# Seven half-size products for eight behind the attention of a gated hybrid block, with fused token steps

## The chip, the cores and the metric

The kernel runs on one core of a Trainium2 chip (trn2). The metric is the device time of one execution, in microseconds (us); lower is better. The engines are TensorE (PE; its weight loads are shown apart as PEld), VectorE (DVE), ScalarE (ACT), GpSimd (POOL) and SyncE (SP), which issues the DMAs of this kernel. Each engine works through its own queue in order; semaphores order the queues among each other.

## The reference, cut to what matters

The input is x of 2048 tokens by 1024 features, the output has the same shape, all float32.

```python
h = rms_norm(x, norm_gain)
proj = h @ w_in                                # 1024 x 8448
qa, ka, va, qb, kb, vb, ga, gb, mg = split(proj)
ya = banded_attention(qa, ka, va, window 128, sink) * silu(ga)    # 512 wide
yb = (three dilated groups of attention, joined by their denominators) * silu(gb)   # 512 wide
gates = sigmoid(mg + b_merge)                  # two gates, each 1024 wide
merged = gates[0] * (ya @ w_branch_a) + gates[1] * (yb @ w_branch_b)
out = x + merged @ w_out
```

## The kernel before

**Precision.** Every large product is made of float16 parts. An operand is split into a high part (`XH`, `wh`) and a low part (`XL`, `wl`), and each product is three matmuls, high by high, high by low and low by high. The high part is a scaled copy by ACT (`w_hi`, L215), the low part is a subtraction by DVE (`w_lo`, L221). `XH` and `XL` hold h transposed, with the features on partitions, and stay in SBUF through the gates.

**Stages.** First x is loaded, normed and turned (`x_turn` L447, `x_hi` L450, `x_lo` L454), and gate chunks 0 and 1 run on the way. Then come 14 attention units of 8 steps each (112 steps, `NPAIR`). Two are A units, twelve are B units. A step does the projections of two sets of 128 tokens (`Pair`, matmuls at L617), their head norms (L635 to L699), the logits (L767), the softmax (`maxima` L782, `exps` L790, `hi` L795, `lo` L799) and the values (L816). `a_merge` and `b_merge_q` join the results, and `YPart` turns 512 tokens of 128 features, multiplies them with the silu gate (L882), takes their maximum (L887) and stores them in DRAM (`ytd`).

**Fills.** A gate chunk is 128 columns of the gate weights, a whole chunk being four quarters of 24 matmuls of 512 columns (`g_step`, L288). Chunks 0 to 7 are the silu gates: a tanh by ACT (L350) and a product by DVE (L357), stored in `gtd` and loaded again by `YPart.load`. Chunks 8 to 11 are merge gates (tanh at L353 only, stored in `mgd`) for output column blocks 6 and 7. The list `FILLS` says in which of the 112 steps a quarter runs between the attention's products, and chunk 8 has steps 116 and 118, behind the attention:

```python
FILLS = ((2, None, (2, 3, 4, 5)), (3, 0, (8, 9, 10, 12)), (4, 1, (17, 19, 20, 21)), ...
```

A chunk needs its own weight preparation: load, gain by POOL (L303), square, norm (L173 and L180 to L188), high and low part (L329, L333).

**The order by hand.** The queues hold what the program emits, in the order of emission. `at(t, f)` puts a piece of work on a heap under a planned time, counted in steps; `until(t)` emits what is due. PE's products are emitted in sequence, and the work of the other engines falls between them as the heap says.

**Behind the attention.** The merge gates of block 0 run in plain order (`mg_step`). All of y is loaded from DRAM and split into `YH` and `YL` (L1122 to L1124). Then, for output blocks dc = 1 to 7 and 0, and for four quarters of 512 tokens each, PE makes the two merge gates (only for dc 1 to 5; the others come from `mgd`) and the two branch products of 12 matmuls each, DVE joins them (L1204, L1205, L1208), and the result is stored in DRAM (`mtd`):

```python
tproj(ps, wh, wl, 256, q, 4, YH, YL, 4 * k)
V.scalar_tensor_tensor(gs[k][:], gs[k][:], 1.0, ps[:], OP.add, OP.mult)
```

The output stage loads `mtd` into `M` and makes 2 x 16 products of 24 matmuls (L1254); DVE adds x (L1257), and SyncE stores the result.

Of the kernel before, what the change touches and what calls it, by code (L numbers as in the profile page):

```python
# [39 lines left out]
VSC = 2.0 ** -20  # L40
SX = 2.0 ** 10
# [31 lines left out]
G_PREP = (5.907, 6.8, 7.032, 7.43, 7.58, 7.73, 7.88)  # L73
# [9 lines left out]
FILLS = ((2, None, (2, 3, 4, 5)), (3, 0, (8, 9, 10, 12)), (4, 1, (17, 19, 20, 21)), (5, 2, (24, 25, 26, 27)), (6, 3, (33, 35, 36, 37)), (7, 4, (40, 41, 42, 44)), (9, 6, (58, 59, 60, 62)), (10, 7, (64, 65, 66, 68)), (11, 10, (88, 89, 90, 92)), (8, 13, (116, 116, 118, 118)))  # L83
# [8 lines left out]
def block_kernel(tc, x, w_units, w_gate, w_mrg, w_out, w_bra, gain, qkg, sink, bias_a, bias_b, b_merge, out):  # L92
# [10 lines left out]
    wp = es.enter_context(tc.tile_pool(name="wp", bufs=2))  # L103
# [43 lines left out]

    def w_load(u, parts=(0, 1, 2, 3)):
        if u not in wtiles:
            wtiles[u] = [raw_tile()]  # L150
        raw = wtiles[u][0]
        src = w_units[u] if u < NU else w_mrg[u - NU]
        for i in parts:
            nc.sync.dma_start(out=raw[:, 2 * i:2 * i + 2, :], in_=src[:, 2 * i:2 * i + 2, :])
# [36 lines left out]
    def w_square(u, i):  # L191
        raw = wtiles[u][0]
        if i == 0:
            wtiles[u] += [wp.tile([128, NCH, 384], F16, name="wh"), wp.tile([128, NCH, 384], F16, name="wl"),
                          sm.tile([128, 4], F32, name="wsq")]
# [64 lines left out]
    ytd = [dr.tile([128, S], F32, name=f"ytd{c}") for c in range(8)]  # L260
    gtd = [dr.tile([128, S], F32, name=f"gtd{c}") for c in range(8)]
    mgd = {k: dr.tile([128, S], F32, name=f"mgd{k}") for k in (0, 1, 12, 13, 14, 15)}
# [4 lines left out]
    gp = main.enter_context(tc.tile_pool(name="gp", bufs=1))  # L267
# [37 lines left out]
    def g_square(c):  # L305
        pool = gp if c > 1 else sp0
        bufs = 1 if c > 1 else 2
        gh = pool.tile([128, NCH, 128], F16, name="gh", bufs=bufs)
        gl = pool.tile([128, NCH, 128], F16, name="gl", bufs=bufs)
# [26 lines left out]
    def g_step(c, q):  # L336
# [3 lines left out]
        m = None if c < 8 else 4 + c  # L340
        ps = pj_p.tile([128, 512], F32, name="pj")
        return tproj_list(ps, gh, gl, 0, q), gate_steps(ps, c, q, ih, m)

    def gate_steps(ps, c, q, ih, m):
# [10 lines left out]
        def gate():  # L355
            if m is None:
                V.scalar_tensor_tensor(th[0][:], th[0][:], 1.0, ps[:], OP.add, OP.mult)  # L357

# [677 lines left out]
    for c, u, slots in FILLS:  # L1036
        for q, k in enumerate(slots):
            fill.setdefault(k, []).append((g_step, c, q))
        if c == 2:
            continue  # L1040
# [293 lines left out]
```

## Time and profile before

| | |
|---|---|
| median of 3 runs | 2015.74 us (2012.35 to 2018.49) |
| span of the profiled execution | 2015.2 us |
| PE busy | 1965.1 us, 98% of the span, 17666 matmuls |
| DVE busy | 1265.5 us, 63% |
| ACT busy | 1004.8 us, 50% |
| POOL busy | 839.3 us, 42% |
| DMA | 276.97 MB, mean 137 GB/s |

No other time is known for the profiled execution than its span from the first to the last instruction. The page cuts the span into 40 slices of 50.4 us; each digit is a busy share in tenths. In a group of instructions the columns are the sum of the busy time, the mean in ns of one, and the idle time of the engine before them with what ended it. In a table of windows each engine has its busy time in that stretch and the number of its instructions; the last three columns are PE's granted clock (1.00 is full), the share of the DMA engines and their rate. The attention's steps lie between about 82 and 1384 us; what is behind them is called the tail.

### The profile page before, as it was taken

Reading aid. Unit: us, or ns where it says so; the run is one execution under the profiler, and the core shown is the slowest. Engines: PE = TensorE matmul, PEld = TensorE weight load, DVE = VectorE, ACT = ScalarE, POOL = GpSimd, SP = SyncE. Lnnn points to the kernel's source line nnn. Section 1 sums busy time; section 2 is a strip of 40 time slices with the busy share of each in tenths; the row PEclk is TensorE's granted clock in tenths of the full one; section 3 lists DMA queues with packets and bytes.
Section 4 is the critical chain, followed back from the end, with each engine's and each line's share of the span. In section 5 each row is a group of like instructions: output and inputs, shape, how many; then the busy total and the mean of one; then the engine's idle time right before and its main releaser. Section 6 shows DMA issues by size and latency. Waiting matters only on the chain.

```text
span 2015.2 us, 47585 instructions
## 1 busy us (share of the span) xinstructions
PE 1965.1 (98%) x17666; PEld 1399.8 (69%) x17666; DVE 1265.5 (63%) x3456; ACT 1004.8 (50%) x2357; POOL 839.3 (42%) x2351
## 2 busy tenths in 40 slices
PE   6999999999999999999999999999999999999999
PEld 4567886678878898788989889896434444444444
DVE  6678877887768876677767877668572322254211
ACT  6467656765655566555666556565362221121100
POOL 4254556455647665566666666666200000000000
PEclk8999999999999999999999999999999999999999
DMA  6249976896659687486966857567551110046832
GB/s 243 79 92 175 171 151 142 152 191 142 167 117 174 134 162 155 97 178 119 183 118 133 183 119 160 99 140 169 149 182 42 48 49 31 27 141 205 268 122 89
DMA packets 560249, 276.97 MB, mean 137 GB/s; under 512 B 457744, under 2 KB 512144, under 8 KB 558480
## 3 DMA queue, kind: packets, MB, share of 16 engines
q1 hardware_dynamic: 560016, 273.93, 59.8%
q8 instruction: 138, 2.26, 0.5%
q14 instruction: 95, 0.78, 0.1%
HBM read 115.23 MB, written 48.50 MB: 81 GB/s over the span
## 4 chain that ended last, share of the span: by engine, by line
PE 79%; POOL 5%; DMA 5%; DVE 5%; issue 4%; ACT 2%; SPq 0%; POOLq 0%; DVEq 0%; ACTq 0%
PE pj L617 32%; PE fps L288 15%; PE pj L288 14%; PE fps L1254 8%; PE s L767 4%; PE pv L816 4%; DVE rw L677 1%; POOL rs_t L249 1%; POOL rs_t L250 1%; POOL rw L684 1%; DVE qss L665 1%; DMA fg<-ytd 1%; POOL rs_t L251 1%; PE s L447 1%; DMA graw<-in_w_gate_dram 1%
## 5 line engine op out<-in xcount | busy, mean ns | idle before, releaser
L617 PE MATMUL pj<-wl,XH 128*128 128x128 f16 (+2 forms) x2816 | 714.6, 268 | 0.0
L617 PE MATMUL pj<-wh,XH 128*128 128x128 f16 (+2 forms) x2816 | 708.4, 268 | 4.0 <-DVE vt L653 4.0
L617 PE MATMUL pj<-wh,XL 128*128 128x128 f16 (+2 forms) x2816 | 712.2, 269 | 0.0
L617 PEld LDWEIGHTS <-XH 128*128 128x128 f16 x5632 | 577.8, 113 | 66.8 <-issue 4.7
L617 PEld LDWEIGHTS <-XL 128*128 128x128 f16 x2816 | 316.8, 113 | 26.0
L782 DVE CUSTOM_DVE_ANT_0 pr<-s,b,ubuf 128x256 f32<-128x256 f32 (+3 forms) x512 | 218.7, 464 | 63.9 <-PE s L767 62.0
L288 PEld LDWEIGHTS <-wh 128*128 128x128 f16 x1280 | 125.7, 99 | 153.7 <-issue 7.7
L249 POOL TENSOR_TENSOR rs_t<-rs_y 128x8 f32<-128x8 f32 (+2 forms) x345 | 108.4, 314 | 209.1 <-DVE rs_y L240 151.8
L799 DVE SCALAR_TENSOR_TENSOR p<-pr,p 128x512 f16<-128x512 f32 (+2 forms) x256 | 184.2, 719 | 6.4 <-ACT p L795 5.3
L159 POOL TENSOR_TENSOR wraw<-wraw,gn 128x768 f32<-128x768 f32 (+1 forms) x80 | 108.3, 1360 | 170.5 <-DMA wraw<-in_w_mrg_dram 170.3
L684 POOL TENSOR_TENSOR rw<-rw,g 128x128 f32<-128x128 f32 (+1 forms) x224 | 137.8, 635 | 82.0 <-DVE rw L677 67.7
L1204 DVE SCALAR_TENSOR_TENSOR fg<-fg,fps 128x512 f32<-128x512 f32 x64 | 43.4, 685 | 202.7 <-PE fps L288 187.2
L677 DVE TENSOR_TENSOR rw<-rw,qr 128x512 f32<-128x512 f32 (+1 forms) x112 | 114.7, 1024 | 87.7 <-POOL vt L646 56.0
L795 ACT ACTIVATE p<-pr 128x512 f16<-128x512 f32 (+2 forms) x256 | 159.1, 622 | 11.0 <-DMA pt<-p 4.7
L635 ACT ACTIVATE rw<-pj 128x256 f32<-128x256 f32 (+1 forms) x224 | 86.6, 386 | 140.5 <-PE pj L617 136.5
L767 PE MATMUL s<-kq 128*128 128x128 f16 (+1 forms) x1856 | 147.3, 218 | 2.8 <-DMA kq<-spl 2.8
L767 PEld LDWEIGHTS <-kq 128*128 128x128 f16 x2016 | 130.1, 98 | 25.1 <-issue 3.0
L288 PE MATMUL pj<-XH,gh 128*128 128x512 f16 x384 | 146.9, 382 | 0.0
L288 PE MATMUL pj<-XL,gh 128*128 128x512 f16 x384 | 146.8, 382 | 0.0
L288 PE MATMUL pj<-XH,gl 128*128 128x512 f16 x384 | 146.6, 382 | 0.0
L699 POOL COPY spl<-spl 128x256 f16<-128x256 f16 (+1 forms) x224 | 92.6, 443 | 126.2 <-DVE spl L694 121.6
L816 PEld LDWEIGHTS <-pt 128*128 128x128 f16 x3024 | 122.0, 97 | 24.3 <-DMA pt<-p 2.4
(182 smaller groups left out, 3644.9 us busy)
## 6 DMA issues: line engine op xcount, KB each, us to landing
wraw<-in_w_units_dram SPq DMA_DIRECT2D x56, 384.0 KB, 4.8
wraw<-in_w_mrg_dram SPq DMA_DIRECT2D x24, 384.0 KB, 4.3
zd<-z SPq DMA_DIRECT2D x128, 66.0 KB, 1.9
zz<-zd SPq DMA_DIRECT2D x64, 132.0 KB, 3.1
xt<-in_x_dram SPq DMA_DIRECT2D x16, 512.0 KB, 9.7
gtd<-yo SPq DMA_DIRECT2D x32, 256.0 KB, 3.1
yo<-gtd SPq DMA_DIRECT2D x32, 256.0 KB, 3.8
ytd<-yo SPq DMA_DIRECT2D x32, 256.0 KB, 4.1
```

The costliest lines, as they stand in the source:

```text
L159: G.tensor_tensor(v, v, gn[:, c0:c0 + 2].unsqueeze(2).to_broadcast([128, 2, n]), OP.mult)
L249: G.tensor_tensor(tv, yv, yv, OP.mult)
L288: out.append(lambda w=w, xx=xx, ch=ch, i=i: T.matmul(ps[:], lhsT=w[:, ch, c0:c0 + 128], rhs=xx[:, ch, ts], start=(i == 0), stop=(i == n - 1)))
L617: out.append(lambda lhs=lhs, rhs=rhs, ch=ch, a=a, b=b, k=k: T.matmul(ps[:, a:b], lhsT=lhs[:, ch, :], rhs=rhs[:, ch, a:b], start=(k == 0), ...
L677: V.tensor_tensor(q, q, self.rr[:, :n].unsqueeze(2).to_broadcast([128, n, HD]), OP.mult)
L684: G.tensor_tensor(q[:, i, :un.nq, :], q[:, i, :un.nq, :], g, OP.mult)
L767: T.matmul(self.sv[j][:, o:o + k1 - k0], lhsT=q[:, h, :], rhs=kt[:, un.nq + kh + v * un.nk, k0:k1], start=(v == 0), stop=(v == 1))
L782: V.tensor_tensor_reduce(out=self.pv[:, j, self.p0:self.p0 + W], in0=self.sv[j], in1=un.bias[:, self.h0 + j, self.b0:self.b0 + W], scale=I ...
L795: A.activation(self.sp[:, :128 * n], self.pr, AF.Copy, scale=PSC)
L799: V.scalar_tensor_tensor(self.sp[:, 128 * n:], self.pr, PSC, self.sp[:, :128 * n], OP.mult, OP.subtract)
L816: T.matmul(self.po[:, j, :w], lhsT=p[:, n * j + s, :], rhs=un.v[key][:, vh, c0:c0 + w], start=(k == 0 and s == 0), stop=(k == 2 and s == n ...
L1254: T.matmul(ps[:], lhsT=m[:, ch, k, 128 * t:128 * t + 128], rhs=woh[h][w][:, ch, :], start=(i == 0), stop=(i == 23))
```

## The change

Every large product behind the attention is written in blocks of two by two, and the four output blocks are made of seven half-size products in place of eight (Winograd's form of Strassen's scheme). With A the data and B the weights, the sums are

S1 = A21 + A22, S2 = S1 - A11, S3 = A11 - A21, S4 = A12 - S2, and T1 to T4 alike of B.

For the gates the blocks of A are the two halves of the tokens by the two halves of the features. The sums are made in float32 and then split into high and low parts, so a product remains three matmuls for each 128 features. Three PSUM banks take the seven products: three products begin a bank, the other four are added onto what a bank holds, and ACT (`copy`) or DVE (`sum`) reads a bank between two of them. The seventh product of a group is emitted behind the first product of the next.

- The list `FILLS` goes. Silu chunks 2 to 7 and the merge gates of blocks 6 and 7 run in the tail; only chunks 0 and 1 stay ahead of the attention. `YPart` of chunks 2 to 7 only copies (by ACT) and stores.
- The tail begins with merge gates 0 and 1 in eight blocks (`Std`), while DVE, POOL and ACT make the sums of h (`s_build`). Sixteen groups of seven follow (`SEQ`): merge gates 2 to 6 (`GateS`) and the six silu chunks (`SiluS`, two to a group), which load y from DRAM, gate it and store it again. Merge gate 7 is again `Std`.
- The branch and the output products run in eight token steps of two times 128 tokens. A step s has two groups with matmuls of 128 columns (`Branch`, one for each branch) and one of 512 columns (`Out`). The y of a step is loaded, summed and split by `y_build`, the merged result stays in SBUF and is summed and split by `m_build`; `mtd` goes. All merge gates are in `mgd`, loaded by `g_tiles`.
- Some scales differ (`SX`, `VSC` and others), so that sums stay in the range of float16. Pools lie on other sides of SBUF.

```diff
-FILLS = ((2, None, (2, 3, 4, 5)), ...)
 class YPart: gate()
         held[0] = False
+        if self.chunk > 1:
+            A.activation(self.o[:], self.ps[:], AF.Copy)
+            return
...
+    PROD = (("A11", 0), ("S1", 2), ("A12", 1), ("S2", 0), ("S4", 2), ("S3", 0), ("A22", 0))
+    MM, MM1 = 2.59, 1.335
...
+    def s_build(q, ch):
...
+        return ((0, lambda: new(0, l21, l22, OP.add, G)), (.1, lambda: new(5, l11, l21, OP.subtract, G)),
+                (.2, lambda: new(3, h11, h21, OP.subtract, G)),
+                (1, lambda: new(1, h21, h22, OP.add)),
+                (3, lambda: more(1, r[0][:], OP.add)), (3.1, lambda: hi(0, 1)),
+                (4, lambda: more(3, r[5][:], OP.add)), (4.1, lambda: hi(2, 3)),
+                (5, lambda: new(2, r[1][:], h11, OP.subtract)), (6, lambda: more(2, l11, OP.subtract)),
+                (6.1, lambda: hi(1, 2)), (7, lambda: lo(0, 1)), (8, lambda: lo(2, 3)),
+                (9, lambda: new(4, h12, r[2][:], OP.subtract)), (10, lambda: more(4, l12, OP.add)),
+                (10.1, lambda: hi(3, 4)), (11, lambda: lo(1, 2)), (12, lambda: lo(3, 4)))
...
+    class Seven:
+        def mm(self, i):
+            k = PROD[i][1]
+            if i < 3:
+                self.b[k] = bank()
+            return self.matmuls(i, self.b[k], i < 3)
+        def after(self, i):
+            b, r = self.b, self.r
+            if i == 0:
+                self.copy(0, b[0])
+            elif i == 1:
+                self.copy(2, b[2])
+            elif i == 2:
+                self.sum(0, b[1])
+            elif i == 3:
+                self.copy(1, b[0])
+            elif i == 4:
+                self.sum(1, b[2])
+            elif i == 5:
+                self.sum(2, b[0])
+            else:
+                self.last(b[0])
...
+    def run(g):
+        emit(g, 0)
+        if pending:
+            emit(pending.pop(), 6)
+        if g.n == 7:
+            for i in range(1, 6):
+                emit(g, i)
+            pending.append(g)
...
+    for q in range(2):
+        for ch in range(4):
+            for d, f in s_build(q, ch):
+                at(7.5 * (4 * q + ch) + 12.0 * q + .61 * d, f)
+    SEQ = ((2, 0), (3, 0), (2, 1), (3, 1), (8, 0), (8, 1), (9, 0), (9, 1), (10, 0), (10, 1), (4, 0), (4, 1),
+           (5, 0), (6, 0), (5, 1), (6, 1))
...
+            run(Std(1, k, q))
+    for dc, q in SEQ:
+        run(GateS(dc, q) if dc < 8 else SiluS(dc - 8, q))
...
+            G.tensor_tensor(s1, a21, a22, OP.add)              # y_build, and m_build alike
+            G.tensor_tensor(s2, s1, a11, OP.subtract)
+            G.tensor_tensor(s4_, a12, s2, OP.subtract)
+            G.tensor_tensor(s3, a11, a21, OP.subtract)
+        def split(i):
+            yf[s, k, i] = f = yp.tile([128, 2, 2, 128], F16, name=f"y{k}")
+            A.activation(f[:, 0], r[1][i], AF.Copy, scale=ysg[:])
+            V.scalar_tensor_tensor(f[:, 1], r[1][i], ysg[:], f[:, 0], OP.mult, OP.subtract)
...
+        def out(self, j, r, d):                                # Branch
+            g = self.g(*((0, 0), (0, 1), (1, 1))[j])
+            at(now[0] + d, lambda: G.tensor_tensor(g, g, r[:], OP.mult))
+            if self.k:
+                self.merge(*((0, 0), (0, 1), (1, 1))[j], d + 1.2)
...
+    g_tiles(0, 0)
+    for p in range(4):
+        wo_build(p, b0 + .5 + 5.6 * p)
...
+    AB(0)                                                      # AB(s): loads, then Branch(s, 0), Branch(s, 1)
+    AB(1)
+    for s in range(8):
+        if s < 6:
+            p = pos[0]
+            at(p, g_tiles, s + 2, 0)
+            y_build(s + 2, 0, p + 6.0)
+            y_build(s + 2, 1, p + 15.0)
+        run(outs[s])
+        if s < 6:
+            AB(s + 2)
```

`w_sums` makes T1 to T4 on POOL; `s_prep`, `wb_build` and `wo_build` call it and split the seven forms of the gate, branch and output weights by ACT and DVE. The numbers in `at` are planned times in us in the tail.

More of the change, by code (lines that the diff above doesn't have):

```diff
@@ L39 @@
 PSC = 2.0 ** 14
-VSC = 2.0 ** -20
-SX = 2.0 ** 10
+VSC = 2.0 ** -16
+SX = 2.0 ** 9
 SE = S + 256
@@ new lines, in std_prep, with part, m_store, m_gate @@
+    def std_prep(dc, b):
+        u = NU + dc
+        def part(i, k):
+            if (u, "n") not in wtiles:
+                wtiles[u, "n"] = 1
+                wtiles[u] += split_tiles(u)
+            (w_hi, w_lo)[k](u, i)
+        for i in range(4):
+            at(b + 1.2 * i, part, i, 0)
+            at(b + 1.0 + 1.2 * i, part, i, 1)
+    def m_store(t, k, dc, t0):
+        nc.sync.dma_start(out=mgd[k, dc, :, t0:t0 + 512], in_=t)
+    def m_gate(dst, src, dc, k, im, t0, d):
+        at(now[0] + d, lambda: A.activation(dst, src, AF.Tanh, bias=bmh[:, 8 * k + dc:8 * k + dc + 1], scale=im[:]))
+        at(now[0] + d + .8, lambda: V.tensor_scalar(dst, dst, 1.0, None, OP.add))
+        at(now[0] + d + 1.3, m_store, dst, k, dc, t0)
@@ L1260, in block_kernel @@
+    pos[0] += .3
+    flush()
+    until(1e9)
+    order.close()
+    rt.close()
+    tl.close()
     es.close()
```

654 lines of the change are left out of this document (464 added, 190 removed).

## The prediction

> **What bounds the kernel now.** I read the page first, then the windows of TensorE (PE) along the span, then the timeline of PE.
>
> ```profile
> span 2015.2 us, 47585 instructions
> PE 1965.1 (98%) x17666; PEld 1399.8 (69%) x17666; DVE 1265.5 (63%) x3456; ACT 1004.8 (50%) x2357; POOL 839.3 (42%) x2351
> PE   6999999999999999999999999999999999999999
> DVE  6678877887768876677767877668572322254211
> PEclk8999999999999999999999999999999999999999
> PE 79%; POOL 5%; DMA 5%; DVE 5%; issue 4%; ACT 2%; SPq 0%; POOLq 0%; DVEq 0%; ACTq 0%
> ```
>
> PE is never out of work after the first slice, and its clock is full. The chain that ends last is PE for 79%. VectorE (DVE) is at 6 to 8 tenths up to slice 28, where the attention ends, and at 1 to 5 tenths behind it. So matmuls that vanish shorten the kernel one for one, as long as no other engine has been hiding behind them. The second question is the whole difficulty here.
>
> The profiled execution's span is 2015.2 us, 0.5 us under the median of the three runs (2015.74); I make the sum against 2015.2 and take the two as one number. About 0.3% (6 us) is what a measurement of this kernel can tell from no change.
>
> **The PE sum.** A busy matmul record overlaps its neighbours, so the price is the distance of starts:
>
> ```profile
> 899.63 0.38 PE L288 MATMUL pj<-XH,gh 128*128 128x512 f16 x1
> 899.85 0.38 PE L288 MATMUL pj<-XL,gh 128*128 128x512 f16 x1
> ...
> 900.28 0.22 PE L617 MATMUL pj<-wh,XH 128*128 128x128 f16 x1
> ...
> 901.57 0.22 PE L617 MATMUL pj<-wh,XL 128*128 128x128 f16 x1
> 901.62 0.27 PE L617 MATMUL pj<-wh,XH 128*128 128x256 f16 x1
> ```
>
> A 512-wide matmul takes 0.216 us (899.63 to 900.28 is three of them, the middle ones are not all shown). Twenty-four 128-wide ones, each with a weight load of its own, lie between 900.28 and 901.62: 1.34 us, 55.8 ns each.
>
> Before, from the loops: twelve gate chunks x 4 x 24 = 1152, merge chunk 0 192, merge chunks 1 to 5 960, branch products 768, output products 768; 3840 matmuls of 512 columns. After: two gate chunks 192, merge chunks 0, 1 and 7 eight-block 576, sixteen seven-product groups x 7 x 12 = 1344, output 8 x 7 x 12 = 672; 2784 of 512 columns. The branch products become 8 x 2 x 7 x 24 = 2688 of 128 columns. So 1056 x 0.216 = 228 us go, 2688 x 0.0558 = 150 us come: **-78 us of PE**. This is a count; whether the sevenths are really saved is not in doubt. The rest of the sum is what takes some of it back.
>
> The 150 us stand on a run of only 24 matmuls. The Trainium skill, TensorE: Matmul & The Clock Gate, section "Back-to-back issue gap", gives about 81 ns as the sustained spacing for 128 columns with a weight load each, and 131 ns for 512; the trace shows neither (55.8 and 216 ns). By that rule the branch products would cost 68 us more. I take the trace's row.
>
> **The attention loses its filling work.** Ten of the gate chunks ran as 24-matmul fills between the attention's products (36 of their 40 quarters inside the attention's steps). Their PE time (5.18 us each) goes from there: 187 us. That counts in full only where DVE, ScalarE (ACT) and POOL can follow the faster steps. The windows over the heaviest stretches, and over stretches without fills:
>
> ```profile
> core 0: us, PE busy (x) PEld busy (x) DVE busy (x) ACT busy (x) POOL busy (x), PEclk, DMA share, GB/s
> 126.60:243.00 116.40, 115.30 (x1413) 88.58 (x1412) 97.05 (x238) 84.68 (x177) 56.08 (x132) 1.00 0.89 161
> 161.00:187.70 26.70, 25.60 (x340) 19.20 (x339) 23.73 (x61) 22.22 (x47) 14.40 (x33) 1.00 1.13 179
> 350.50:483.30 132.80, 132.59 (x1462) 98.62 (x1461) 110.33 (x273) 92.57 (x201) 67.54 (x161) 1.00 0.91 168
> 386.00:411.90 25.90, 25.69 (x340) 19.09 (x339) 23.92 (x61) 22.03 (x47) 14.36 (x33) 1.00 1.07 190
> 616.80:687.10 70.30, 69.78 (x792) 58.23 (x791) 58.21 (x183) 36.43 (x92) 48.41 (x129) 1.00 0.71 143
> 885.10:954.70 69.60, 69.57 (x790) 58.22 (x790) 56.50 (x179) 36.91 (x93) 45.69 (x121) 1.00 0.71 148
> 1133.90:1207.40 73.50, 71.35 (x792) 59.53 (x790) 59.81 (x181) 37.48 (x94) 49.54 (x131) 0.98 0.65 140
> 1056.40:1073.90 17.50, 17.50 (x235) 16.38 (x233) 11.61 (x40) 9.37 (x29) 10.15 (x37) 1.00 0.82 198
> ```
>
> The reader sees a DVE that is at 83% in the A units *with* fills in them (97.05 of 116.4, 110.33 of 132.8). The two stretches 161.0 to 187.7 and 386.0 to 411.9 are A steps without fills: DVE at 89% and 92%, and PE still hardly waits. So 92% is what DVE is known to reach. What the change takes off DVE is in these rows, with the others that later parts use:
>
> ```profile
> L677 DVE TENSOR_TENSOR rw<-rw,qr 128x512 f32<-128x512 f32 x96 | 95.8, 998 | 82.3 <-POOL vt L646 50.6 <-POOL qr L252 22.3 <-POOL vw L646 9.2
> L1208 DVE SCALAR_TENSOR_TENSOR mm<-fg,ubuf,mm 128x512 f16<-128x512 f32 x32 | 24.0, 751 | 16.6 <-ACT mm L1207 16.5
> L882 DVE SCALAR_TENSOR_TENSOR yo<-pt,ubuf,yo 128x512 f32<-128x512 f32 x32 | 23.8, 744 | 4.7 <-DMA yo<-gtd 3.4 <-PE pt L878 1.3
> L350 ACT ACTIVATE yo<-pj,ubuf 128x512 f32<-128x512 f32 x32 | 22.0, 688 | 34.0 <-PE pj L288 33.8
> L357 DVE SCALAR_TENSOR_TENSOR yo<-yo,pj 128x512 f32<-128x512 f32 x32 | 21.9, 685 | 16.5 <-ACT yo L350 16.2
> L887 DVE TENSOR_REDUCE ymx<-yo 128x1 f32<-128x512 f32 x32 | 21.7, 677 | 0.1
> L454 DVE TENSOR_TENSOR XL<-s,XH 128x512 f16<-128x512 f32 x32 | 21.6, 686 | 8.5 <-ACT XH L450 8.4
> L333 DVE SCALAR_TENSOR_TENSOR gl<-wraw,ubuf,gh 128x1024 f16<-128x1024 f32 x9 | 11.7, 1298 | 0.3 <-ACT gh L329 0.3
> L183 DVE TENSOR_SCALAR pw_p<-wm 128x1 int32<-128x1 int32 x43 | 6.6, 153 | 1.4
> ```
>
> A silu fill takes 0.685 (L357) with it, a chunk's weight preparation 1.30 (L333) and about seven small operations of 0.15 (L183); the gating of an output part of chunks 2 to 7 0.744 + 0.677 (L882, L887; ACT takes a copy of at most 0.69 instead, by L350, and loses the tanh). Stretch by stretch, PE after, DVE after, DVE at 92%:
> - 126.6 to 243.0, five fills: PE 116.4 - 25.9 = 90.5; DVE 97.05 - 3.4 - 2.3 = 91.3; 99.2. Lost: 8.7.
> - 350.5 to 483.3, six fills, four parts: PE 101.7; DVE 110.33 - 4.1 - 2.3 - 5.7 = 98.2; 106.8. Lost: 5.1.
> - 616.8 to 687.1: 49.6; 58.21 - 2.05 - 2.3 - 4.3 = 49.6; 53.9. Lost: 4.3.
> - 885.1 to 954.7, whose fills are merge gates without L357: 48.9; 49.9; 54.2. Lost: 5.3.
> - 1133.9 to 1207.4: 52.8; 53.2; 57.8. Lost: 5.0.
>
> Together 28. Next to each stretch lie steps such as 1056.4 to 1073.9, with DVE at 66%, where a backlog of some 2 us is made up; five times that leaves **+17 us**. Bounds: 0 (PE waits as little as at 386.0), and 59 if DVE only reaches 85% (17 + 14 + 9 + 10 + 10). The nearest rows are the two without fills, hence the low half. The fills' DMAs (weights, gate stores and reloads) leave SyncE's queue and POOL's weight gains leave POOL; that costs nothing, since neither ended a PE wait there.
>
> **Behind the attention** PE has the same kind of work as before, but DVE, ACT and POOL get the sums, splits and recombinations. What before lost there, and its quiet stretch:
>
> ```profile
> 1432.00:1500.00 68.00, 60.10 (x285) 27.34 (x284) 42.64 (x102) 36.20 (x68) 8.71 (x11) 0.92 0.55 180
> 1600.00:1700.00 100.00, 100.00 (x468) 45.66 (x467) 26.92 (x55) 24.11 (x43) 4.07 (x4) 1.00 0.12 40
> 1840.00:1848.00 8.00, 5.89 (x20) 2.21 (x19) 2.44 (x4) 0.67 (x1) 0.00 (x0) 0.79 0.73 245
> ```
>
> At 0.216 us, 285 matmuls are 61.5 us of the 68 and 20 are 4.3 of the 8: 10 us lost, and gone with their stages. In their place:
>
> *Sums of h.* 83 DVE tensor_tensor operations with both sources in SBUF (88 in all) must be done before the third group's second product, some 80 us into the tail, with 14 weight splits of 0.751, sums and +1 steps, about 22 us. At 0.686 the 83 are 57 us: 79 of 80 us, no loss. But POOL computes 24 of the sums and the weights' sums beside them, and:
>
> ```profile
> 107.07 1.47 POOL L159 TENSOR_TENSOR wraw<-wraw,gn 128x768 f32<-128x768 f32 x1
> 107.11 2.11 DVE L677 TENSOR_TENSOR rw<-rw,qr 128x640 f32<-128x640 f32 x1 [3.37 <-POOL vt L646]
> ```
>
> this DVE operation began 0.04 us behind a POOL one and ended 0.68 us after it: it stood still meanwhile. Hence the mean of 998 ns for L677 against 686 for L454, which reads PSUM. At 998 the 83 take 26 us more, 25 late. Bounds 0 and 25; POOL is less busy here than where 998 was measured, I take +13. The Trainium skill, SBUF — State Buffer, section "SBUF: two separate sides", has the rule for it: DVE with two SBUF inputs and a POOL operation that reads SBUF lock each other out. The trace agrees for tensor_tensor.
>
> *Into the fused token steps.* The gates of two steps (3 MB) are queued on SyncE ahead of the first output weights; at the 245 GB/s of the row 1840 to 1848 they take 12 us, and ACT's and POOL's in-order queues stand behind them. Bounds 3.7 (before's own hand-over) and 13; I take +8.
>
> *Sixteen branch groups.* The sixth product adds onto a bank that ACT must copy out after the fourth, and only one product (1.34 us) lies between; the seventh waits for a DVE sum after the sixth in the same way.
>
> ```profile
> 1602.96 0.38 PE L288 MATMUL fps<-YH,wh 128*128 128x512 f16 x1
> 1603.16 0.78 ACT L1197 ACTIVATE fg<-fps,bmh,ubuf 128x512 f32<-128x512 f32 x1 [4.34 <-PE fps L288]
> ```
>
> Here ACT starts 0.20 us after PE has gone on to the next product. With 0.69 for the copy (L350) that is 0.9 of the 1.34 us: it fits if ACT is free. One more 0.7 us operation ahead, every time, would cost some 0.3 to 0.7 at 32 places, at most 22; bounds 0 and 22, I take +6, since ACT has 27 splits and copies in the 37 us of a token step, at most 0.69 each, so at most 19 us. Behind the waiting matmul stand all later products. *Other joints*, such as the entry from the attention: +6, between 2 and 12, an estimate from the two rows of before's joints. The last store behind the last matmul stays.
>
> Tail: 13 + 8 + 6 + 6 - 10 = **+23 us**. Sum: 2015.2 - 78 + 17 + 23 = **1977 us**.
>
> **The rivals.**
> 1. *The cover was not needed.* DVE follows at 95% and more, and the tail loses only 10 as before: 2015 - 78 + 10 = 1947. For it: PE waits of 0.2 us at 386.0. Against: the lock of DVE and POOL. Chance 0.17.
> 2. *DVE becomes the attention's bound* at 85%: 59 instead of 17, 2019. For it: the A rows. Against: 92% at 386.0. Chance 0.10.
> 3. *Slower: ACT's order in the branch groups.* Copies stand behind splits that wait for POOL. The gain is gone when each of the 32 bank hand-overs costs 38 / 32 = 1.2 us more. With two 0.7 us operations of ACT and half a POOL operation ahead it is 2 us: 64, of which 6 are in the sum, so 1977 + 58 = 2035. For it: POOL's long operations. Against: ACT's 19 us in 37. Chance 0.10.
> 4. *A long run of 128-wide matmuls is held by its weight loads*, one after the other at 99 ns:
>
> ```profile
> L288 PEld LDWEIGHTS <-wh 128*128 128x128 f16 x1280 | 125.7, 99 | 153.7 <-issue 7.7
> ```
>
> 2688 x (0.099 - 0.0558) = 116, so 2093. Against it: the 24 at 55.8 ns, whose loads overlap. Chance 0.03. The rule of the Trainium skill named above (TensorE: Matmul & The Clock Gate) is this rival in a milder form; by it the time would be 2045.
>
> That the change does not save its sevenths is no rival: the counts above are those of the instructions it issues.
>
> **The numbers.** Forecast 0.60, 1977, its own range 1955 to 2002. Faster by over 0.3%: 0.60 + 0.17 + a third of rival 2 = 0.80; same 0.06; slower 0.14. Range 1947 to 2018: rival 3 and 4 stay out, and half of what lies at the fast end.
>
> **What the changed profile would show.** Right: 128-wide branch matmuls at 55 to 56 ns; the A steps without fills at DVE 90% and more with PE waits for L653's successors of a few us; a PE dip about 45 to 85 us into the tail, with DVE named; another at the first token step with a DMA named. Wrong: branch spacing near 81 ns, waits of over 1 us at most branch products, or an attention more than 40 us longer than its matmuls.

## The result

The changed kernel takes **2135.8 us** (median of four, 2134.6 to 2139.6) against 2017.1 us (four, 2012.4 to 2019.6) for the kernel before on the same chip: **1.0594 times as long, 95% interval 1.0576 to 1.0612**. The forecast was 1977 and its range ended at 2018. The count of matmuls was right. What was wrong is the price of the waits that take it back: 40 us in the forecast, 201 us on the chip.

The profiled execution took 2139.6 us, its span 2136.9. The page, with the first lines and the slices:

```profile
span 2136.9 us, 52081 instructions
PE 1946.8 (91%) x19278; PEld 1474.4 (69%) x19278; DVE 1556.7 (73%) x3698; ACT 1186.3 (56%) x2743; POOL 1136.9 (53%) x2587
PE   6999999999899998999889999869999994799899
DVE  6589869967887688767887677884674568756764
POOL 4255555656666667656666665440110247656653
PEclk9999999999999999999999999979999996899999
```

PE has holes in many slices where it had none before, the deepest at the 27th slice (6 tenths) and at the 34th and 35th (4 and 7), and the clock drops beside them. DVE stays at 4 to 8 tenths behind the attention, where it was at 1 to 5 but for one slice of 7.

The windows by stage (us, then busy time of PE, PEld, DVE, ACT, POOL with counts, granted clock, DMA share, GB/s), first after, then before:

```profile
81.00:1272.00 1191.00, 1124.00 (x13469) 1004.75 (x13468) 926.39 (x2642) 756.29 (x1923) 748.08 (x2206) 0.98 0.73 143
1272.00:1336.00 64.00, 57.84 (x402) 30.31 (x401) 48.37 (x140) 30.14 (x68) 35.09 (x59) 0.95 0.59 138
1336.00:1436.00 100.00, 75.16 (x320) 32.70 (x319) 91.42 (x130) 55.67 (x108) 40.83 (x28) 0.89 0.18 63
1436.00:1755.00 319.00, 313.46 (x1539) 146.19 (x1538) 187.23 (x348) 169.39 (x328) 64.96 (x64) 0.99 0.35 116
1755.00:1856.00 101.00, 55.45 (x605) 46.85 (x603) 79.37 (x80) 40.73 (x72) 74.33 (x54) 0.74 0.41 126
1856.00:2136.90 280.90, 258.82 (x2628) 175.99 (x2626) 167.65 (x230) 81.80 (x155) 147.59 (x122) 0.95 0.38 112
```
```profile
82.00:1384.00 1302.00, 1285.86 (x14359) 1079.02 (x14358) 978.76 (x2835) 795.72 (x1965) 765.79 (x2223) 1.00 0.73 146
1384.00:2015.20 631.20, 616.79 (x2982) 283.08 (x2979) 228.22 (x483) 154.77 (x300) 44.97 (x70) 0.99 0.37 117
```

The attention is 111 us shorter, not 187; the tail takes 865 us instead of 631, of which 109 (187 - 78) are matmuls that moved there or were added on balance. For the table I summed, from the trace, how far each matmul's start lies behind the one before it beyond 0.2157, 0.1625, 0.1094 and 0.0557 us for 512, 384, 256 and 128 columns; time at half clock counts in it. This is what "waits" means below.

| place | forecast, more than before | waits before | waits after |
|---|---|---|---|
| attention | +17 | 30 | 106 |
| joint behind it (1272 to 1336) | +6, with other joints | 18 in the whole tail | 10 |
| sums of h (1336 to 1451) | +13 | - | 35 |
| groups up to the token steps (1451 to 1755) | - | - | 8 |
| into the fused token steps (1755 to 1856) | +8 | - | 58 |
| output and branch steps (1856 to the end) | +6 | - | 33 |

201 more, less the 78 of PE, is 123; the spans differ by 122. The matmul waits by what ended them (line waited at, releaser, us in total, times, longest):

```profile
PE fps L1618 <- ACT t L1349: 26.3, 5, 7.9
PE fps L1692 <- DVE xr L1699: 25.5, 8, 7.1
PE fps L1369 <- ACT t L1349: 25.3, 5, 9.6
PE s L770 <- DMA kq<-spl: 23.0, 12, 4.5
PE pj L620 <- DVE vt L656: 17.1, 10, 3.8
PE fps L1618 <- DVE t L1353: 12.1, 3, 6.5
```

L1618 are branch products, L1692 output products, L1369 seven-product gates; L1349 is the copy that frees a bank. Five of the six releasers are elementwise operations in an in-order queue. The sixth is a transfer (`kq<-spl`, 23.0 us), and its source `spl` is written by two such operations (L697 and L702 below).

### The profile page after: what moved, and what is told of

Same layout as the page of the kernel before. It is cut to its first block, busy times and chain, and to the rows that moved or that the text cites. A ratio compares the mean times of both kernels' runs of the same rounds, so it can differ in the third digit from the quotient of the medians.

```text
span 2136.9 us, 52081 instructions
## 1 busy us (share of the span) xinstructions
PE 1946.8 (91%) x19278; PEld 1474.4 (69%) x19278; DVE 1556.7 (73%) x3698; ACT 1186.3 (56%) x2743; POOL 1136.9 (53%) x2587
## 5 line engine op out<-in xcount | busy, mean ns | idle before, releaser
L620 PE MATMUL pj<-wh,XH 128*128 128x128 f16 (+2 forms) x2816 | 718.9, 271 | 17.2 <-DVE vt L656 17.1
L620 PE MATMUL pj<-wl,XH 128*128 128x128 f16 (+2 forms) x2816 | 725.2, 271 | 0.0
L693 ACT ACTIVATE spl<-rw 128x512 f16<-128x512 f32 (+1 forms) x112 | 72.2, 645 | 233.7 <-POOL vt L649 200.4
L1618 PE MATMUL fps<-y,bigh 128*128 128x128 f16 x1792 | 164.1, 227 | 38.4 <-ACT t L1349 26.3
L1369 PEld LDWEIGHTS <-wh 128*128 128x128 f16 x896 | 89.4, 100 | 141.1 <-issue 41.5
L702 POOL COPY spl<-spl 128x256 f16<-128x256 f16 (+1 forms) x224 | 89.5, 429 | 177.5 <-DVE spl L697 175.0
L1618 PEld LDWEIGHTS <-bigh 128*128 128x128 f16 x1792 | 146.4, 102 | 45.2 <-issue 41.4
L1692 PE MATMUL fps<-WOh,mf 128*128 128x512 f16 x448 | 146.9, 401 | 25.5 <-DVE xr L1699 25.5
L798 ACT ACTIVATE p<-pr 128x512 f16<-128x512 f32 (+2 forms) x256 | 159.3, 622 | 17.9 <-DMA pt<-p 10.4
L1618 PE MATMUL fps<-y,bigl 128*128 128x128 f16 x896 | 161.6, 226 | 0.0
L1692 PEld LDWEIGHTS <-mf 128*128 128x128 f16 x672 | 67.7, 102 | 109.9 <-issue 42.6
L819 PE MATMUL pv<-vt,pt 128*128 128x65 f16 (+1 forms) x2784 | 134.1, 194 | 9.9 <-DMA pt<-p 8.9
```

The lines of the kernel that those rows point to most:

```text
L620: out.append(lambda lhs=lhs, rhs=rhs, ch=ch, a=a, b=b, k=k: T.matmul(ps[:, a:b], lhsT=lhs[:, ch, :], rhs=rhs[:, ch, a:b], start=(k == 0), ...
L798: A.activation(self.sp[:, :128 * n], self.pr, AF.Copy, scale=PSC)
L819: T.matmul(self.po[:, j, :w], lhsT=p[:, n * j + s, :], rhs=un.v[key][:, vh, c0:c0 + w], start=(k == 0 and s == 0), stop=(k == 2 and s == n ...
L1369: out.append(lambda w=w, lo=lo, ch=ch, k=k: T.matmul(ps[:], lhsT=w[:, i, ch, :], rhs=xform(f, lo, ch, self.q), start=(fresh and k == 0), s ...
L1618: out.append(lambda p=p, c=c, wl=wl, yl=yl, n=n: T.matmul(ps[:, 128 * p:128 * p + 128], lhsT=w[wl][:, i, c, p, :], rhs=y[:, yl, c, :], sta ...
L1692: out.append(lambda p=p, ml=ml, wl=wl, k=k: T.matmul(ps[:], lhsT=m[:, ml, p, :], rhs=WO[wl][:, i, p, :], start=(fresh and k == 0), stop=(k ...
```

## Experiments

Times come from different chips, on which the kernel before took 2017 to 2021 us; so each is given as median and ratio to the kernel before. A difference of 0.001 in the ratio is 2 us. The changed kernel is at 1.0594.

**The attention: is it the missing fills?** `e1_silu_fills` puts six of the ten filled chunks back:

```
+FILLS = ((2, None, (2, 3, 4, 5)), (3, 0, (8, 9, 10, 12)), ..., (7, 4, (40, 41, 42, 44)))
-    SEQ = (..., (8, 0), (8, 1), (9, 0), (9, 1), (10, 0), (10, 1), ...)
+    SEQ = ((2, 0), (3, 0), (2, 1), (3, 1), (4, 0), (4, 1), (5, 0), (6, 0), (5, 1), (6, 1))
```

> One part undone: the six silu gates (chunks 2 to 7) are computed in the attention again, as 24 fills of 24 matmuls at the old places, and are gated there as before; the three silu groups of the tail go. Merge chunks 6 and 7 stay in the tail as seven-product groups. TensorE gets 24 x 5.18 = 124 us in the attention and loses 6 x 18.1 = 109 us behind it. Theory (the attention lost its cover: the matmul waits there rose from 30 to 106 us because the fills are gone): the waits fall by about 55, the attention takes about 1191 + 124 - 55 = 1260 us, the kernel about 2097. Rival (the waits come from other things that changed in the attention, such as the copies that replaced the gating, pools and weights): they stay at about 106, the attention takes 1315, the kernel 2152.

Measured 2101.9, ratio 1.0412 (1.0395 to 1.0428). The attention takes 1268 us with 59 us of waits. Its fills reach up to step 44, so one kernel holds both cases. Units B1,1 (with fills again) and B2,1, B3,1 (still without; B units are named by their two indices in the program), windows after and then in this kernel:

```profile
540.90:635.40 94.50, 83.33 (x1109) 80.42 (x1108) 78.68 (x227) 53.64 (x138) 65.37 (x183) 0.95 0.72 138
787.50:879.40 91.90, 81.79 (x1109) 80.44 (x1107) 76.10 (x225) 53.87 (x138) 62.61 (x177) 0.96 0.68 143
1029.60:1123.90 94.30, 83.03 (x1109) 80.59 (x1107) 77.59 (x227) 51.92 (x134) 64.56 (x182) 0.95 0.66 129
```
```profile
615.30:714.60 99.30, 98.58 (x1205) 86.95 (x1204) 80.54 (x242) 54.97 (x138) 66.70 (x182) 1.00 0.78 151
865.80:957.20 91.40, 80.69 (x1109) 79.07 (x1108) 80.69 (x232) 51.92 (x134) 62.26 (x176) 0.98 0.81 152
1108.00:1203.30 95.30, 84.17 (x1108) 81.13 (x1107) 83.65 (x237) 50.08 (x131) 65.38 (x184) 0.93 0.71 140
```

In B1,1 PE is busy 98.6 of 99.3 us; 96 matmuls of 512 (20.7 us) cost only 4.8 us of span. In the two other units little changed, although their output parts are gated on DVE as before again, not copied by ACT (DVE 80.7 us, not 76.1, in B2,1). So the rival fails, and the lost fills are the cause of the 47 us of waits that went with their return (106 to 59). Yet DVE is at 83% in these units, not at the 92% at which I had let it become the bound.

**What binds at 83%?** The timeline of one step of B1,1 after, POOL and then DVE (start, duration; a bracket is idle time and its releaser):

```profile
548.07 0.20 POOL L254 TENSOR_TENSOR rs_t<-rs_y 128x8 f32<-128x8 f32 x1 [0.54 <-DVE bm_d L972]
551.66 0.20 POOL L257 TENSOR_TENSOR qr<-rs_t,rs_y 128x8 f32<-128x8 f32 x1
551.82 2.20 POOL L982 TENSOR_TENSOR zz<-zz,bm_e 128x256 f32<-128x256 f32 x3
554.31 1.05 POOL L687 TENSOR_TENSOR rw<-rw,g 128x128 f32<-128x128 f32 x2
558.27 0.74 POOL L702 COPY spl<-spl 128x256 f16<-128x256 f16 x2 [2.86 <-DVE spl L697]
551.90 1.08 DVE L680 TENSOR_TENSOR rw<-rw,qr 128x512 f32<-128x512 f32 x1 [0.57 <-POOL qr L257]
553.49 0.82 DVE L988 TENSOR_TENSOR ya<-zz 128x256 f32<-128x256 f32 x1 [0.51 <-POOL zz L982]
557.52 0.69 DVE L697 TENSOR_TENSOR spl<-rw,spl 128x512 f16<-128x512 f32 x1
```

A loop through two in-order queues: Newton steps for the roots of the head norms (POOL, 548.07 to 551.86), scale (DVE), merge products (POOL, 2.2 us, of the unit before), gain (POOL), low parts (DVE), swap (POOL); the next step's Newton steps begin at 559.56. The loop takes 11.5 us, 13.4 with the weight gains in it; neither engine is full, and both wait for each other in every round. Most steps with a fill are longer than that and hide it; without, it sets the pace. Three experiments shorten it. `e5_merge_order` moves the products into POOL's idle 2.9 us and the sums L988 behind L697:

```
-B_MERGE = (-0.037, 0.133, 0.333, 0.507, 0.665, 0.991)
+B_MERGE = (-0.037, 0.133, 0.333, 0.507, 1.015, 1.341)
```

> Two numbers changed: in the B units' merge the three products on GpSimd are put 0.35 of a step later (behind the query gain, ahead of the swap, where GpSimd idles 2.5 us) and the sums on VectorE 0.35 later (behind the low parts of q and k). Theory (not a full engine but a loop holds the units B1,1, B2,1 and B3,1: each step runs once round statistics on VectorE, Newton steps on GpSimd, scale on VectorE, the 2.2 us of merge products on GpSimd, gain, low parts on VectorE, swap; the loop takes 11.5 to 13.4 us and the step's matmuls less now that the fills are gone): the loop gets 2.2 us shorter, of the 49 us of waits in these three units some 25 to 30 go, 2136 - 27 = 2109. Rival (VectorE is full at 87%, the order doesn't matter): less than 8 us, 2128 or more.

`e12_gain_scalar` takes four POOL operations of 1.5 us a unit away:

```
     def w_gain(u, i):
-        gains(wtiles[u][0], 2 * i, 384 if u < NU else 256)
+        raw, n = wtiles[u][0], 384 if u < NU else 256
+        for c in range(2 * i, 2 * i + 2):
+            A.activation(raw[:, c, :n], raw[:, c, :n], AF.Copy, scale=gn[:, c:c + 1])
```

> In the attention the gain on a unit's raw weights (four GpSimd operations of 1.5 us a unit) goes to ScalarE, as eight operations of some 0.6 us. Everything else is the changed kernel. Theory (in the units that lost their fills the loop of VectorE and GpSimd is too long for a step, and these operations lengthen it and lock VectorE): the waits of the attention fall from 106 by some 15, 2136 - 15 = 2121. Rival (VectorE alone is full): within 6 us of 2136. Third (ScalarE's eight operations stand in the way of the exponents): slower.

`e14_loop_both` does both.

> The changed kernel with the edits of e5_merge_order (19 us faster than the changed kernel) and e12_gain_scalar (25 us) together. Theory (both shorten the same loop of VectorE and GpSimd, at different places, and the loop still is longer than a step): they nearly add, 40 us, 2096. Rival (they take the same slack twice): 28 us or less, 2108 or more.

Measured: 2117.3 (1.0496, 1.0470 to 1.0523), 2110.7 (1.0449, 1.0424 to 1.0475) and 2087.9 (1.0348, 1.0324 to 1.0372). By the ratios 20, 29 and 50 us: they add. The rounds show where the time goes. Four of them in a row in B1,1, from one start of the Newton steps to the next, take 11.5, 13.4, 13.3 and 11.1 us in the changed kernel (from 548.07). With the merge order alone they take 10.9, 12.9, 12.9 and 10.3, with the gains on ACT 11.5, 11.1, 11.9 and 11.2, with both 10.9, 10.3, 10.4 and 10.3. The three units with both edits:

```profile
535.10:619.20 84.10, 78.79 (x1109) 77.77 (x1108) 71.20 (x224) 57.62 (x146) 57.91 (x176) 1.00 0.83 154
766.60:850.00 83.40, 78.53 (x1108) 77.63 (x1107) 70.53 (x223) 57.39 (x146) 57.50 (x175) 1.00 0.75 158
997.30:1080.90 83.60, 78.58 (x1109) 77.65 (x1108) 70.65 (x223) 55.64 (x142) 57.72 (x175) 1.00 0.74 143
```

Waits of 49 us in these units became some 20 with the same matmuls, and the clock is full. DVE is now at 85% there, so 83% was not its limit. Alone, the merge order took 13 of the hoped-for 25 to 30 us there, since it shortens a round by 0.4 to 0.8 us and not by 2.2. The gains alone took 7 there, and 18 in the other units of the attention. Units A0 and B0,1 keep 23 of their 25 us; what holds them is open.

**The sums of h.** POOL computes 24 of them. `e4_s_dve` gives these to DVE (`new(0, l21, l22, OP.add, G)` without `G`, and two more like it):

> The 24 sums of h that GpSimd computes go to VectorE. Theory (a GpSimd operation that reads SBUF stops VectorE operations with two SBUF inputs, so GpSimd's help is worth nothing): VectorE gets 24 x 0.69 = 16.5 us more and loses about 14 of the 19 us by which its sums were lengthened, the time stays within 6 us of 2136. Rival (the help is real, and VectorE is simply full): 12 to 16 us slower, 2150. Third (the sums wait for GpSimd's queue): 10 us faster.

2135.9, ratio 1.0583 (1.0568 to 1.0599): 16 us of work moved onto the busier engine at no cost. DVE's busy time in this stretch even fell, from 91.42 us:

```profile
1336.00:1436.00 100.00, 74.91 (x309) 32.32 (x308) 89.78 (x147) 56.37 (x110) 16.72 (x12) 0.85 0.16 56
```

POOL's help was worth nothing. `e6_std2` gives the sums 41 us more time by computing chunk 2 in eight blocks; `e11_std2_weights_later` is e6 and asks for chunk 3's weights 12 us later; `e13_sums_spread` is e11 and issues the sums evenly:

```
+    for q in range(4):
+        for k in range(2):
+            run(Std(2, k, q))                                    # e6; SEQ without chunk 2
-        ready = b + 8.0
+        ready = b + (20.0 if dc == 2 else 8.0)                   # e11
-                at(7.5 * (4 * q + ch) + 12.0 * q + .61 * d, f)
+                at(12.5 * (4 * q + ch) + .95 * d, f)             # e13
```

> Merge chunk 2 is computed in eight blocks ahead of the first seven-product group, as chunk 1 is; TensorE gets 192 - 168 = 24 matmuls of 512 more, 5.2 us, and the sums of h get 41 us more before their first use. Theory (VectorE cannot finish the sums in time; the four waits of 25 us at 1380 to 1435, the one of 4 us at 1511 and their half clock, 35 us in all, are the sums of h): some 28 us go, 2136 + 5 - 28 = 2113. Rival (it is the weights of the first groups and ScalarE's order): the waits move to the new first group, 2135 to 2142.

> As e6_std2 (chunk 2 in eight blocks, 2124.5), with the weights of chunk 3 asked for 12 us later, so that TensorE's small matmul for their norm no longer stands 20.5 us in its queue ahead of the groups. Theory (e6_std2 took away the waits for the sums of h and put one wait of its own in their place): 20 us and the half clock behind it go, 2124.5 - 22 = 2102. Rival (VectorE's lateness comes back as a wait at the first seven-product group): 2115 or more.

> As e11_std2_weights_later (2117.6), with the sums of h issued at an even pace over the 100 us before the last of them is due (12.5 us for a group of operations, 7.5 and a pause before); no operation is added or left out. Theory (the sums were put into the queues faster than VectorE can work, and ScalarE's copies that free a bank stood behind splits whose sums were not ready: an order effect): the waits of 8.5 us at 1420 and 4.8 at 1528 and their half clock go, 2117.6 - 14 = 2104. Rival (VectorE is full, 92% from 1340 to 1420, and the pace of issue changes nothing): within 5 us of 2117.6.

Measured 2124.5 (1.0540, 1.0505 to 1.0574), 2117.6 (1.0486, 1.0462 to 1.0510) and 2116.8 (1.0488, 1.0470 to 1.0506). In e6 the waits for banks went but for one of 4.3 us, and one wait of 20.5 us of my own making came: the small matmul for chunk 3's norm stood in PE's queue. In e11 and e13 some 15 us of waits for banks are left; the rival that I had named held both times, and e6 itself lay midway between theory and rival. ScalarE's waits in the changed kernel (1336 to 1436) show how DVE's lateness reaches PE:

```profile
ACT bigh L1177 <- DVE t L1174: 38.3, 21, 3.7
```

The splits of h stand in ACT's queue ahead of the copies that free banks, and wait for sums; DVE is busy 91.4 us of these 100. Chunk 2 in eight blocks makes the kernel 22 us shorter (e11) although it adds 5.2 us of matmuls: here one saved seventh had cost five times its worth in waits. An even pace changes nothing: DVE has too much to do there, whatever the order.

**Into the token steps.** `e3_y_first` puts the next step's y ahead of 12 gate loads and the output weights (in `AB(0)`: the `load`s at `p` and `p + .01`, not at `p + 5.5` and `p + 14.8`).

> The loads of the second token step's y (two parts) are issued at the start of the first token step, ahead of the 12 gate loads and the output weights, not 5.5 and 14.8 us later behind them. Sums and splits keep their places. Theory (SyncE's queue: the first waits of the token steps, 7.7 us at 1761 and what follows it, come from these loads standing behind 3 MB of gates and behind output weights that wait for a free buffer): the 7.7 us and their half clock go, and GpSimd's and ScalarE's idle 12 to 14 us there are used, 2136 - 20 = 2116 (bounds 2105 and 2126). Rival (GpSimd and VectorE have more work than the two steps last, so that an earlier start of the y only moves the wait behind it): 2130 or more.

2132.3, ratio 1.0569 (1.0547 to 1.0591): 5 us, not clear of the noise, and the rival held. One of the seven long waits at the entry went, 4 us of its 58; the first is no shorter (8.4 us, before 7.7). When y no longer waits, ScalarE's first output-weight split stands in its queue ahead of the copies instead, for its own transfer (in this run):

```profile
1763.49 0.72 ACT L1584 ACTIVATE WOh<-xr,ubuf 128x512 f16<-128x512 f32 x1 [8.76 <-DMA xr<-in_w_out_dram]
```

`e7_no_wo_sums` is without the sixteen POOL sums:

```
-            r.append(w_sums(*raw, lambda t: t[:], t2))
+            r.append(((raw[0], raw[1], raw[2], raw[3], raw[3], raw[1], raw[2]), [lambda: None] * 4))
```

> The 16 sums on GpSimd from which the output weights' forms are made are left out (the forms take unsummed weights, so the output is not the reference's); loads, the 28 high and 28 low parts and everything else stay. Theory (at the entry into the token steps GpSimd and, through the lock, VectorE and ScalarE's order behind them hold the branch products): 16 x 1.6 us of GpSimd go and the low parts fall from 1.19 to 0.75 us, of the 53 us of waits in 1760 to 1856 and their half clock about half goes, 2136 - 25 = 2111. Rival (the 28 splits themselves fill VectorE and ScalarE): 2128 or more.

2118.7, ratio 1.0501 (1.0475 to 1.0526): waits of 58 us became 44, between the theory and its rival. The low parts still take 1.04 us each in this run. I put the rest down to the splits themselves. By form in the changed kernel (1755 to 1856):

```profile
L1587 DVE SCALAR_TENSOR_TENSOR WOl<-t,ubuf,WOh 128x512 f16<-128x512 f32 x16 | 18.7, 1190 | 0.0
L1587 DVE SCALAR_TENSOR_TENSOR WOl<-xr,ubuf,WOh 128x512 f16<-128x512 f32 x12 | 16.7, 1401 | 0.0
L1353 DVE TENSOR_TENSOR t<-fps,t 128x512 f32<-128x512 f32 x11 | 7.4, 680 | 2.6 <-PE fps L1618 2.6
L1207 POOL TENSOR_TENSOR t<-xr 128x512 f32<-128x512 f32 x4 | 6.6, 1646 | 0.0
```

28 low parts at 1.19 to 1.40 us are 35 us of DVE in two token steps of 18.7 us of branch matmuls each, and the sums of the branch products, on which a bank depends, stand among them.

**The output steps.** `e2_m_late` puts the splits of m later, nothing else:

```
-            at(b + d, split, i)          # m_build
+            at(b + d + 9.0, split, i)
```

> One number changed: the seven splits of the merged m in m_build are put 9 us later into the queues of ScalarE and VectorE (the sums on GpSimd stay where they are). Theory (in each of five output steps one matmul waits 3.53 us, and the clock is halved for some 4 us behind it, because the add that frees its bank stands in VectorE's queue behind m and y splits that are not due yet): five times 5.5 us go, 2136 - 28 = 2108. Rival (VectorE has too little time there whatever the order): the splits then stand in front of another add or sum, 2130 to 2140. Third: mf or g buffers come free later and the loads of the next gates are held, slower than 2140.

2110.3, ratio 1.0459 (1.0440 to 1.0479). The wait in five output steps, after (DVE's queue, then PE):

```profile
1938.94 0.74 DVE L1665 SCALAR_TENSOR_TENSOR mf<-t,ubuf,mf 128x512 f16<-128x512 f32 x1
1939.60 0.47 DVE L1547 SCALAR_TENSOR_TENSOR y<-bigl,ubuf,y 128x256 f16<-128x256 f32 x1
1940.00 0.74 DVE L1699 SCALAR_TENSOR_TENSOR xr<-fps,ubuf,xr 128x512 f32<-128x512 f32 x1
...
1937.04 0.38 PE L1692 MATMUL fps<-WOh,mf 128*128 128x512 f16 x1
1940.79 0.59 PE L1692 MATMUL fps<-WOh,mf 128*128 128x512 f16 x1 [3.37 <-DVE xr L1699]
1941.17 0.63 PE L1692 MATMUL fps<-WOl,mf 128*128 128x512 f16 x1
...
1945.86 0.42 PE L1618 MATMUL fps<-y,bigh 128*128 128x128 f16 x2
```

The add that frees the bank (1940.00) stands behind splits of m and y for later steps. Twelve matmuls then take 5.07 us (1940.79 to 1945.86) instead of 2.59: half clock. With the splits later the same wait is 1.4 to 1.9 us, and its twelve matmuls run at 0.216. Of the 27 us, 18 are waits that went here; another 8 went at the entry, where the first splits of m stand.

**All at once, and the token steps alone.** `e8_combined` is e1, e2, e5 and e6 together; `e9_tokens_alone` keeps the attention of before and merge chunks of eight blocks and has only the branch and output products in sevens; `e10_tokens_stored` is e9 with the output weights' forms made during chunks 1 to 4, kept in DRAM and loaded, with the second step's y loaded ahead of its gates, and with m's splits later; `e15_best` is e10 with both loop edits.

```
+            f = t2()[:].bitcast(F16)                              # e10, in chunks 1 to 4
+            A.activation(f[:, :512], r[0][0][i], AF.Copy, scale=so[:])
+            V.scalar_tensor_tensor(f[:, 512:], r[0][0][i], so[:], f[:, :512], OP.mult, OP.subtract)
+            at(now[0] + 1.0, lambda: nc.sync.dma_start(out=wod[i, p], in_=f))
...
+        nc.sync.dma_start(out=WO[i][:], in_=wod[i].rearrange("p r (k n) -> r p k n", k=2))
```

> Four edits at once: silu gates as fills in the attention (e1_silu_fills), chunk 2 in eight blocks, the merge products later, m's splits later (e2_m_late). If the causes are separate places their gains add: 2102 (silu fills, measured) - 27 (late m, measured against the kernel after) - 23 (chunk 2) - 15 (merge order, for the two units that are still without fills) = 2037. If one engine's total is the bound, the sum does not add up and it stays above 2060.

> One part of the change alone: the branch and output products in seven blocks and fused token steps. All ten fills are back in the attention, the merge chunks 2 to 5 are in eight blocks as before, there are no sums of h. The weights of the branch products are formed during those chunks, the output weights as in the changed kernel. TensorE against the kernel before: 15.7 us less for the branch, 20.7 less for the output products. Theory (three separate places of loss: attention, sums of h, token steps): the attention is that of before, 1302 us; the tail is 627 - 18 (its waits) - 36 + 60 (entry) + 28 (five output steps) + 5 = 666, the kernel 2015 + 39 = 2054. Rival (the waits in the token steps are a legacy of work left over from the groups ahead of them): they go with those groups, 1985 to 2000.

> As e9_tokens_alone, and the work that stands in the way at the entry is done earlier: the forms of the output weights are made during chunks 1 to 4, where VectorE and GpSimd have little to do, kept in DRAM and loaded form by form (7 MB) in the first two token steps; the second step's y is loaded ahead of its gates; m's splits come 9 us later as in e2_m_late. Theory (the entry's 60 us are the forming of the output weights: sums, splits and the lock, and 28 us in the output steps are m's place): the entry costs 5 to 10, the output steps 10; tail 627 - 18 - 36 + 8 + 10 + 5 = 596, the kernel 2015 - 31 = 1984, below the kernel before. Rival (transfers: some 12 MB in the first two steps at 290 GB/s are 41 us of 37): the first output step waits for its weights 10 us or more, 1995 to 2005. Second rival (VectorE and ScalarE are full in the token steps anyway): 2030.

> e10_tokens_stored (2002.9, ratio 0.9916 to the kernel before) with the edits of e5_merge_order and e12_gain_scalar. Theory (the fills cover the loop, so that only some 27 us of waits are left in the attention): 3 to 8 us faster, about 1997. Rival (ScalarE's eight operations a unit cost more than they free): 2003 to 2010.

- e8: 2075.7, ratio 1.0286 (1.0256 to 1.0316). The gains do not all add (2037 was expected): late m does, chunk 2 brings its norm matmul's wait again (17.9 us), and the merge order gave nothing in the two units without fills (31 us of waits, 32 in e1). Rounds of 11.1 us became 10.3 there, but others 0.4 to 0.9 us longer; why is open. These two items are 33 of the missing 39 us, so that one engine's total need not be the bound, although the time stayed above the 2060 I had set for that.
- e9: 2058.8, ratio 1.0197 (1.0173 to 1.0222). The waits in the token steps are their own: 57 at the entry, 31 behind it, with nothing left over from other groups.
- e10: **2002.9, ratio 0.9916 (0.9891 to 0.9941)**. The entry, first in e9 and then here (a stretch with 776 matmuls, not 568):

```profile
1680.00:1778.00 98.00, 54.11 (x568) 45.76 (x566) 77.20 (x78) 40.74 (x72) 73.26 (x52) 0.72 0.40 122
```
```profile
1674.00:1743.00 69.00, 59.02 (x776) 47.32 (x775) 42.79 (x58) 26.44 (x51) 49.92 (x42) 0.97 0.83 256
```

DVE's 77 us became 43, the waits 57 became 14 (33 and 9 over the same matmuls as in e9); 256 GB/s carry the weights in. Several edits were made at once. Alone, the earlier y took 4 us off these waits (e3) and the later splits of m 8 (e2), so most of the fall is the forming, if they add. It missed 1984, since 18 us of waits between the attention and the token steps stayed (I had allowed 5), and the entry took 14, not 8.
- e15: **1996.1, ratio 0.9887 (0.9867 to 0.9907)**, faster than the kernel before by 23 us and the fastest of all here. Its 6 us below e10 are not clear of the noise.

## Why the prediction was wrong

- **The PE sum** (-78) held. The branch products run at 55.8 ns: 1914.93 to 1922.80 are 141 of them.

```profile
1914.93 0.28 PE L1618 MATMUL fps<-y,bigh 128*128 128x128 f16 x2
...
1922.80 0.28 PE L1618 MATMUL fps<-y,bigh 128*128 128x128 f16 x2
```

Rival 4 and the 81 ns of the Trainium skill (TensorE: Matmul & The Clock Gate, "Back-to-back issue gap") are out: 55.8 ns with a weight load each.
- **"The attention loses its filling work": +17, measured +76.** The failed step is "DVE at 92%" as the one limit. I took it from stretches of A steps, of 26 us each. In the units B1,1, B2,1 and B3,1 the limit is the time round a loop of DVE and POOL, which busy shares do not show; they hold 49 of the 106 us of waits, against 9 before. For the rest, above all A0 and B0,1, no run shows what took the place of this step. My upper bound (59, DVE at 85%) was also too low, and rival 2, which is that bound, came nearest for the wrong reason: DVE reached 78% over the whole attention (926.39 of 1191). The sum had two more faults: 28 less five times 2 is 18 and not 17, and its five stretches hold 23 of the 36 fills; the other 13 were put at nothing without a reason.
- **"Sums of h": +13, measured +35.** The deadline was taken at 80 us; half of the sums are due at the first seven-product group, 41 us after the first of them could start. And I let POOL take 24 sums off DVE, when e4 shows that this takes nothing off it. What helped was a later deadline (e11). The bound 25 was too low as well.
- **"Into the fused token steps": +8, measured +58.** I priced the gate loads and not the forming of the output weights (16 POOL sums, 28 splits on DVE and on ACT): the operations were counted for h and left out here. This is the largest error by ratio. In e10, where that work is done elsewhere, 57 us became 14; by e2 and e3 up to 12 of these 43 belong to the other edits.
- **"Sixteen branch groups": +6, measured +33 in the stage.** The branch groups hardly wait once the weights are formed (no L1618 wait over 0.9 us behind 1830). The output products, for which the sum had no term, do: five waits of 3.5 us and the half clock behind them. Rival 3, one of those that ended slower, named a place nearby; the mechanism, a freeing operation queued behind work that is not due, is real, but it sits on DVE in the output products and on ACT in the seven-product gates.
- **Missing altogether: the clock.** I priced no wait with a second price. Each of 13 long waits that could be looked at alone cost 1.4 to 2.9 us more (see the end).
- The named signs: the dip "45 to 85 us into the tail, with DVE named" came (at 1380, 44 us behind the start of the tail's own groups at 1336, first named ACT and behind it DVE), as did the one at the first token step, there with ACT named and not only a DMA, and an attention "more than 40 us longer than its matmuls", my sign for wrong, came too (76). The sign "DVE 90% and more" in the A units did not: it is at 75% in A0 and 83% in A1.

```profile
81.00:172.30 91.30, 84.86 (x866) 57.75 (x865) 68.13 (x161) 58.97 (x127) 49.21 (x130) 1.00 0.63 120
277.80:373.50 95.70, 91.29 (x1035) 64.66 (x1033) 79.80 (x201) 71.83 (x161) 58.26 (x153) 0.98 0.84 151
```

## What to carry to other kernels

Before fills are taken from a loop, measure how long one round of its helper chain takes through all in-order queues; a step that becomes shorter than this round is paced by it while no engine is full (in B1,1 PE 88%, DVE 83%, POOL 69%). When matmuls are saved by sums and splits, count these against the deadline of the first use, stage by stage, and do what is due late early, in a stage whose engines rest. Put an operation that frees a bank ahead of everything that is not due.

## What the chip showed

- Half clock follows an idle PE. In the changed kernel all 13 waits of 3.3 us and more that had 8 us without another wait behind them were followed by 1.4 to 2.9 us lost at twice the pitch; those under 2 us by less than 0.5 on average. The Trainium skill, TensorE: Matmul & The Clock Gate, "Part 1: The HAM clock gate", gives an idle window of about 3.4 us for this. The trace agrees for the long waits only: of eight waits between 2.1 and 3.3 us, the five from 2.43 us on were followed by 1.4 to 1.7 us of such loss, the three up to 2.34 by 0.2 or less.
- The lock of DVE and POOL also holds for scalar_tensor_tensor with two SBUF inputs, which I had not seen before: L1587 takes 1190 and 1401 ns beside POOL, against 751 for the row L1208 before; L1353, which reads PSUM, stays at 680. It is the rule of the Trainium skill, SBUF — State Buffer, "SBUF: two separate sides", as it is written; I had narrowed it to tensor_tensor. e4 shows what follows here: without the 24 sums on POOL, DVE's own sums L1174 fell from 870 and 966 ns to 685 and 809, and its busy time did not grow.
